# Seven block products for the down projections of a two-layer decoder trunk

## The chip, the cores and the metric

The kernel runs on one core of a Trainium2 chip. The metric is the device time of one execution in microseconds (us). TensorE (PE) multiplies; VectorE (DVE), ScalarE (ACT) and GpSimd (POOL) work on SBUF and PSUM; SyncE (SP) issues most DMAs.

## What is computed

1088 tokens (a prompt of 1024 and 8 samples of 8) go through two layers, each a token mixer and a ConvFFN, and a final norm. Everything is float32. Three of the products go from a wide row back to the 1024 features, and are added to x through a gate that depends on the sequence:

```python
def conv_ffn(h, past, w_up, conv_w, conv_b, w_down):
    a = h @ w_up                                   # 1024 -> 2 x 2816
    conv = sum(conv_w[j] * ap[:, j:j + T] for j in range(CONV_W)) + conv_b
    g, u = jnp.split(conv, 2, axis=-1)
    y = (jax.nn.silu(g) * u) @ w_down              # 2816 -> 1024
...
    out = (u * mixed.reshape(B, T, D_SGU)) @ w_out # 2048 -> 1024 (sgu_mix, layer 1)
...
    x = x + g1 * mix
    x = x + g2 * f                                 # after each mixer, each ConvFFN
```

Layer 0 has attention and a ConvFFN, layer 1 the spatial gating mixer (SGU) and a ConvFFN. So there are three down products: `w_down` of layer 0 (22 row tiles of 128), `w_sgu_out` (16), `w_down` of layer 1 (22).

## The kernel before

Activations lie feature-major: a row tile is 128 features by 1088 tokens. For float32 accuracy each operand is split in two float32r parts, high and low, and a product is three passes: high by high, high by low, low by high (`mm`, L370, issues each matmul; every matmul of the kernel has that line, and the name of its PSUM tile tells the stage: `m` the up product, `acc` the down product, `misc` a last block, `adaps` conditioning).

The up product of an FFN is already done in the seven-product (Winograd) form for all but its first column tiles: two blocks of columns, two of rows and two halves of the tokens make seven products in place of eight, in two parts z of 272 tokens a half. ACT and DVE add them from PSUM (`ev`, `ext`: L1544 to L1567), POOL makes the weights' sums and low parts (L1485 to L1502). Behind each pair of column tiles come the convolution (L1678, L1680, DVE), the gate (L1693) and the store of the row tile in a scratch tensor in DRAM (`pscr`; `sscr` for the SGU).

`Down.run` (L1625) does a down product in blocks of row tiles, `FF_BLOCKS = [4, 4, 4, 4, 2, 4]` and `SG_BLOCKS = [4, 4, 4, 4]`. For each block but the last, `proj_block` (L1196) goes over eight column tiles m of 128 features. A weight unit holds two of them (a *unit* below); it comes by DMA (`raw`), ACT casts it to `whi` (L305), and DVE (POOL for `w_sgu_out`) makes `wlo` (L312). For each m there are three chunks of tokens (384, 384, 320 columns), one PSUM bank each, and 3 passes for each row tile. Then `add_gated_` (L524 to L535) adds the banks to x with the gate, on DVE: one operation per bank and two small ones for the samples (`gs`, `xs`).

The rows of the next block are brought by `load` (L1587): a DMA of the row tile (`p`, L1594), the cast `gh` on ACT (L1596), the rest `gl` on DVE (L1597). The first four are loaded within the last up pair, as `free` gives back the tiles of the norm's rows, after its products 1, 2, 4 and 7; x comes back from `xscr` after the last (L1599). In layer 0 the 48 conditioning units of layer 1 are spread over the units of the first five blocks. The last block is done by `last_block7` (L1411; then another seven-product stage follows) or `last_block` (L1441), chunk by chunk, with the norm of the next stage behind it.

The order of work on each engine follows from the program text and from a priority (`tc.high_priority`) that puts the adds from PSUM ahead; each engine then runs its own queue in order. SBUF tiles of one row tile come from a ring of 37 slots (`slot`), weights from pools `raw` and `w`, PSUM tiles from 8 banks.

## Time and profile before

| | |
|---|---|
| time of three runs | 2646.1, 2651.22, 2651.64 us (median 2651.22) |
| profiled execution: its own time and its span | 2651.8 us, from its first to its last instruction |
| mean granted TensorE clock | 0.982 |
| busy: PE, DVE, ACT, POOL | 97%, 64%, 37%, 51% of the span |
| first down product up to its last block | 961.9 to 1205 us |
| SGU down product up to its last block | 1661.9 to 1810.9 us |
| last down product up to its last block | 2371.3 to 2589.7 us |

A row of a group gives line, engine, operation, `out<-in` by tile names, the shapes and the count, then after the bar the busy time in us and the mean of one in ns, and after the next bar the idle time ahead of it with what ended it. A row of the chain or the timeline gives start, duration, engine and what. A row of the windows gives, for a stretch, the busy time of PE, PE's weight loads, DVE, ACT and POOL with the count of instructions, then the granted clock, the DMA share and GB/s. PE's ends are modelled, so a busy PE is not PE at its peak.

### The profile page before, as it was taken

To read this page: it belongs to the slowest core of one execution; us is meant where nothing else is said; L and a number is where in the kernel's file an instruction comes from. 1 tells how busy PE (TensorE), PEld (TensorE's weight loads), DVE (VectorE), ACT (ScalarE), POOL (GpSimd) and SP (SyncE) were. 2 spreads that over 40 slices of the span, in tenths; PEclk is the share of its full clock that TensorE was granted. 3 is DMA by queue.
4 is the path that set the end of the run, shared out by engine and by line. 5 is a ranking of instruction groups with operands and counts; after the bars stand their busy time and mean duration, and the time that the engine had idled before them with its cause. 6 is when DMAs were issued, how large, how long until landed. Compare 5 with 4: busy or idle time off the path is not lost.

```text
span 2651.8 us, 45949 instructions
## 1 busy us (share of the span) xinstructions
PE 2559.8 (97%) x17916; PEld 2393.3 (90%) x17916; DVE 1687.4 (64%) x3336; ACT 976.8 (37%) x1971; POOL 1358.2 (51%) x1456
## 2 busy tenths in 40 slices
PE   7999999979999999999999999999979999999998
PEld 5676788979999999999788999999879999999998
DVE  5415867877767774446744555655886777766545
ACT  3216853433343331113325655212533343332203
POOL 2315634589999920002543766223489999950002
PEclk9999999989999999999999999999889999999999
DMA  8242213012222265443322434521212222244211
GB/s 295 92 157 97 69 58 120 25 52 80 88 76 74 82 258 189 179 175 130 105 82 78 158 131 160 204 80 64 72 38 78 90 74 74 74 166 176 96 44 68
DMA packets 113945, 292.21 MB, mean 110 GB/s; under 512 B 15329, under 2 KB 47137, under 8 KB 113697
## 3 DMA queue, kind: packets, MB, share of 16 engines
q1 hardware_dynamic: 82016, 232.49, 26.5%
q10 hardware_dynamic: 31712, 56.79, 5.6%
q8 instruction: 142, 2.33, 0.4%
q14 instruction: 75, 0.61, 0.1%
HBM read 228.06 MB, written 63.07 MB: 110 GB/s over the span
## 4 chain that ended last, share of the span: by engine, by line
PE 80%; DVE 11%; POOL 4%; ACT 2%; issue 2%; DMA 1%; SPq 0%; DVEq 0%; ACTq 0%; POOLq 0%
PE m L370 31%; PE acc L370 23%; PE misc L370 8%; PE v L370 7%; PE y L370 5%; POOL w L1485 2%; PE u L370 2%; PE adaps L370 2%; DVE cv L1678 1%; DMA raw<-wts 1%; DVE cv L1680 1%; DVE ha L1348 1%; PE pv L370 1%; ACT P L836 1%; DVE T L1364 1%
## 5 line engine op out<-in xcount | busy, mean ns | idle before, releaser
L370 PE MATMUL m<-th,w 128*128 128x272 f32 x2944 | 568.2, 290 | 25.5 <-ACT ext L1702 18.7
L370 PEld LDWEIGHTS m<-th,w 128*128 128x128 f32 x2944 | 469.8, 190 | 26.3 <-ACT ext L1702 19.1
L370 PE MATMUL m<-tl,w 128*128 128x272 f32 x1472 | 426.9, 290 | 0.0
L531 DVE SCALAR_TENSOR_TENSOR x<-acc,mod,x 128x384 f32<-128x384 f32 (+1 forms) x312 | 159.6, 568 | 239.9 <-PE acc L370 233.8
L370 PE MATMUL m<-hb,w 128*128 128x272 f32 x2208 | 293.2, 289 | 0.0
L370 PEld LDWEIGHTS m<-hb,w 128*128 128x128 f32 x2208 | 284.5, 189 | 0.0
L370 PEld LDWEIGHTS m<-tl,w 128*128 128x128 f32 x1472 | 280.1, 190 | 0.0
L370 PE MATMUL acc<-gh,whi 128*128 128x384 f32 (+1 forms) x1152 | 256.2, 330 | 1.1 <-DVE mixed L1934 0.8
L305 ACT CAST whi<-raw 128x1024 fp32r<-128x1024 f32 (+1 forms) x112 | 113.9, 1018 | 386.8 <-PE acc L370 221.5
L370 PE MATMUL acc<-gl,whi 128*128 128x384 f32 (+1 forms) x1152 | 253.8, 328 | 0.6 <-DVE gl L1597 0.6
L370 PE MATMUL acc<-gh,wlo 128*128 128x384 f32 (+1 forms) x1152 | 253.6, 328 | 0.0
L1295 POOL TENSOR_TENSOR nsq<-nsq 128x544 f32<-128x544 f32 x36 | 55.7, 1547 | 308.2 <-ACT nsq L1288 271.5
L370 PEld LDWEIGHTS acc<-gh,whi 128*128 128x128 f32 x1152 | 195.0, 188 | 10.0 <-issue 5.8
L1485 POOL TENSOR_TENSOR w<-raw,w 128x512 fp32r<-128x512 f32 x138 | 189.1, 1382 | 28.5 <-ACT w L1484 27.2
L370 PEld LDWEIGHTS acc<-gl,whi 128*128 128x128 f32 x1152 | 195.9, 188 | 0.9 <-DVE gl L1597 0.9
L370 PEld LDWEIGHTS acc<-gh,wlo 128*128 128x128 f32 x1152 | 195.8, 188 | 0.0
L1678 DVE SCALAR_TENSOR_TENSOR cv<-ext,cst,cv 128x1104 f32<-128x1104 f32 x88 | 129.0, 1501 | 86.9 <-ACT cv L1677 40.4
L1484 ACT CAST w<-Sa 128x512 fp32r<-128x512 f32 x92 | 56.9, 623 | 309.4 <-POOL Sa L1495 163.1
L1544 DVE TENSOR_TENSOR ext<-ev,m 128x272 f32<-128x272 f32 (+1 forms) x456 | 137.7, 338 | 48.5 <-PE m L370 39.4
L312 POOL TENSOR_TENSOR wlo<-raw,whi 128x1024 fp32r<-128x1024 f32 x28 | 69.7, 2490 | 186.4 <-ACT whi L305 169.3
L1680 DVE SCALAR_TENSOR_TENSOR cv<-ext,cst,cv 128x1104 f32<-128x1104 f32 x88 | 160.9, 1862 | 0.1
L370 PE MATMUL m<-ha,w 128*128 128x272 f32 x1104 | 151.5, 294 | 9.4 <-ACT ext L1702 9.4
(279 smaller groups left out, 5775.3 us busy)
## 6 DMA issues: line engine op xcount, KB each, us to landing
raw<-wts SPq DMA_DIRECT2D x244, 512.0 KB, 3.8
wada<-wts SPq DMA_DIRECT2D x48, 512.0 KB, 4.2
pscr<-cv ACTq DMA_DIRECT2D x44, 544.0 KB, 5.5
p<-pscr SPq DMA_DIRECT2D x40, 544.0 KB, 6.0
xscr<-x ACTq DMA_DIRECT2D x24, 512.0 KB, 2.6
x<-xscr SPq DMA_DIRECT2D x24, 512.0 KB, 8.3
sscr<-mixed ACTq DMA_DIRECT2D x16, 544.0 KB, 3.6
vscr<-v ACTq DMA_DIRECT2D x32, 256.0 KB, 2.6
```

The lines of the kernel that those rows point to most:

```text
L305: nc.scalar.copy(hi[:, :c], r[:, :c])
L312: eng.tensor_sub(lo[:, :c], r[:, :c], hi[:, :c].bitcast(F32))
L370: PE.matmul(out, lhsT=l, rhs=r, start=start, stop=stop)
L531: V.scalar_tensor_tensor(xv, p[:, 0:w], gp, xv, op0=ALU.mult, op1=ALU.add)
L836: A.activation(p, p, AF.Exp, bias=nm[:, h:h + 1], scale=0.125, accum_out=su[:, h:h + 1])
L1295: (V if m == 7 else G).tensor_add(s.ss[z], s.ss[z], q)
L1348: V.scalar_tensor_tensor(lo, t[:, h, 0:w], sh, hi.bitcast(F32), op0=ALU.add, op1=ALU.subtract)
L1484: A.copy(t[:, 0:512], src)
L1485: eng.tensor_sub(t[:, 512:1024], src, t[:, 0:512].bitcast(F32))
L1544: V.tensor_add(o, f(p), f(q))
L1678: V.scalar_tensor_tensor(t[:, 0:1104], e[:, 1:1105], cw(jj * 3 + 1), t[:, 0:1104], op0=ALU.mult, op1=ALU.add)
L1680: V.scalar_tensor_tensor(t[:, 0:1104], e[:, 0:1104], cw(jj * 3), t[:, 0:1104], op0=ALU.mult, op1=ALU.add)
```

## The change

All blocks of the three down products but the last are done as seven block products too. The blocks of one product are two row tiles (A, B), two halves of the tokens, and the two column tiles of a weight unit.

- `Rows` loads a pair of row tiles as `pr`, makes four sums (`tr`, 544 columns each: on DVE for the first pairs, on POOL for the others) and splits seven sides into high and low parts: seven casts on ACT, seven subtractions on DVE (L1590, L1596).
- `weights` makes the seven weights of a unit (a new layout, key `o7`): four sums of 256 columns on POOL (L1659 to L1668), four casts on ACT, four subtractions on DVE of 512, 256, 512 and 512 columns (L1656); half of that for a block of two row tiles. It is a generator, one step of it after each product of the unit before. These units are no longer fetched by `prefetch` or `ahead`.
- `run` does the products of a unit in the order 1, 5, 4, 6, 2, 3, 7, with product 4 put off into the next unit. Each product is two parts z of 272 columns and sums over the block's pairs. Three pairs of PSUM banks are used: `acA` (1, then 6 and 7, and 4), `acC` (5, 3), `acB` (2); a later product goes on in the bank of an earlier one, and the bank is added again after each.
- The banks are added without the gate to `acc`, eight tiles in SBUF: twelve adds of 272 columns on DVE a unit (L1729), and product 1 by a copy on ACT and an add on POOL. In the first block ACT copies the banks of the products that come first.
- `merge` brings x back and adds `acc` with the gate (L1688, and `gs`, `xs`, L1691, L1693), two column tiles a unit in the last seven-product block and two behind it.
- `free` now starts the first pair after product 2 of the last up pair and the second after product 7. The scratch tensors are laid out by halves of the tokens, the SGU's gate writes that layout, and conditioning weights come from the ring of slots. The last blocks are as before.

```diff
-LA, LB = 3, 5
+LA, LB = 1, 2
...
+            if k == "o7":
+                a = a.reshape(nk // 2, 2, 128, 2, 128).transpose(2, 1, 3, 0, 4)
+                a = np.stack([a[:, 0, 0], a[:, 1, 0], a[:, 1, 1], a[:, 0, 1]], 1)
...
+        def make(r):
+            a, b = r.p
+            V_, e = V.tensor_sub, r.e.tensor_sub
+            t1 = slot([128, 2, 544], name="tr")
+            e(t1[:, 0], a[:, 1], a[:, 0])
+            e(t1[:, 1], b[:, 1], t1[:, 0])
+            h0 = slot([128, 2, 544], F32R, name="h0")
+            A.copy(h0[:, 0], a[:, 0])
+            V_(h0[:, 1], a[:, 0], h0[:, 0].bitcast(F32))
...
+            e(t2[:, 0], b[:, 1], a[:, 1])
+            e(t2[:, 1], b[:, 0], t1[:, 1])
...
+            G.tensor_add(S1, A21, A22)
+            parts(f[:, 0:2 * n], 1, 2)
+            yield
+            G.tensor_sub(S2, S1, A11)
+            parts(f[:, 2 * n:3 * n], 4)
+            yield
+            parts(sf[:, 0:2 * n], 5, 6)
+            G.tensor_sub(S4, A12, S2)
+            yield
+            G.tensor_sub(S3, A11, A21)
+            yield
+            parts(sf[:, 2 * n:4 * n], 3, 7)
...
                 elif i == 2:
                     for k in range(1, 8, 2):
                         norm.ab[k][0] = None
-                    s.load(1)
-                elif i == 4:
-                    s.load(2)
+                    s.pair(0, V)
                 elif i == 7:
                     norm.th = norm.tl = None
-                    s.load(3)
-                    s.load_x()
+                    if s.blocks[0] > 2:
+                        s.pair(1, V)
...
+            def add(m, h, b, first, z, e=None):
+                o = s.acc[m][:, h, z * 272:z * 272 + 272]
+                p = b[z][:, 0:272]
+                if first:
+                    A.copy(o, p)
+                elif e:
+                    t = sm.tile([128, 272], F32, name="ev", tag="ev", bufs=4)
+                    A.copy(t, p)
+                    e.tensor_add(o, o, t)
+                else:
+                    V.tensor_add(o, o, p)
...
+                        if i == 1:
+                            product(w, sd, bA, True, lambda z: add(m0, 0, bA, first, z, G))
+                        elif i == 5:
+                            product(w, sd, bC, True, lambda z: add(m1, 1, bC, first, z))
+                        elif i == 4:
+                            while late:
+                                late.pop(0)()
+                            late.append(lambda w=w, sd=sd, bA=bA, m1=m1, first=first:
+                                        product(w, sd, bA, False, lambda z: add(m1, 0, bA, first, z)))
+                        elif i == 6:
+                            product(w, sd, bA, False, lambda z: add(m0, 1, bA, first, z))
+                        elif i == 2:
+                            product(w, sd, bB, True, lambda z: add(m0, 0, bB, False, z))
+                        elif i == 3:
+                            product(w, sd, bC, False, lambda z: add(m0, 1, bC, False, z))
+                        elif i == 7:
+                            product(w, sd, bA, False, lambda z: add(m1, 1, bA, False, z))
...
+                        if i == 4 and b == nb - 2 and u > 0:
+                            s.merge(2 * u - 2)
+                            s.merge(2 * u - 1)
```

How the queues change shows on DVE. First the transition to the third down product: before, the convolution and the gate of the last pair with the loads' subtractions (`gl`) between them, ahead of the last up products' adds (`ev`).

```order
L1678 SCALAR_TENSOR_TENSOR cv<-ext,cst,cv 128x1104 x2
L1680 SCALAR_TENSOR_TENSOR cv<-ext,cst,cv 128x1104 x2
L1597 TENSOR_TENSOR gl<-p,gh 128x1088
L1693 TENSOR_TENSOR cv<-cv 128x1024
L312 TENSOR_TENSOR wlo<-raw,whi 128x1024
L1694 TENSOR_TENSOR cv<-cv 128x64
L1544 TENSOR_TENSOR ext<-ev,m 128x272
L1544 TENSOR_TENSOR ext<-ev,m 128x240
L1544 TENSOR_TENSOR ext<-ev,m 128x4x8
L1597 TENSOR_TENSOR gl<-p,gh 128x1088
L1561 TENSOR_TENSOR ev<-ev,m 128x272 x2
L1565 TENSOR_TENSOR ev<-ev,m 128x272
```

Now, DVE's queue from the first pair's sums (`tr`) on, again up to the adds of the last up products; the convolution's operations come 20 rows further on.

```order
L1586 TENSOR_TENSOR tr<-pr 128x544
L1656 TENSOR_TENSOR w_26887<-raw,w_26887 128x512
L1587 TENSOR_TENSOR tr<-pr,tr 128x544
L1656 TENSOR_TENSOR w_26917<-raw,w_26917 128x256
L1590 TENSOR_TENSOR h_26861<-pr,h_26861 128x544
L1596 TENSOR_TENSOR h_26865<-tr,h_26864 128x544 x2
L1600 TENSOR_TENSOR tr<-pr 128x544
L1602 TENSOR_TENSOR tr<-pr,tr 128x544
L1596 TENSOR_TENSOR h_26874<-pr,h_26873 128x544 x2
L1596 TENSOR_TENSOR h_26880<-tr,h_26879 128x544 x2
L1554 TENSOR_TENSOR ev<-ev,m 128x272 x2
L1656 TENSOR_TENSOR w_26948<-s_26885,w_26948 128x512
```

The first pair's eleven operations and three weight subtractions stand ahead of the last up pair's `ev` adds. The queue goes on with the second pair and the convolution, up to the first unit's adds from `acB`:

```order
L1596 TENSOR_TENSOR h_27043<-tr,h_27042 128x544 x2
L1537 TENSOR_TENSOR ext<-ev,m 128x272
L1537 TENSOR_TENSOR ext<-ev,m 128x240
L1537 TENSOR_TENSOR ext<-ev,m 128x4x8
L1656 TENSOR_TENSOR w_27137<-raw,w_27137 128x512
L1656 TENSOR_TENSOR w_27172<-raw,w_27172 128x256
L1656 TENSOR_TENSOR w_27189<-s_27135,w_27189 128x512
L1656 TENSOR_TENSOR w_27222<-s_27135,w_27222 128x512
L1843 SCALAR_TENSOR_TENSOR cv<-ext,cst,cv 128x1104 x2
L1845 SCALAR_TENSOR_TENSOR cv<-ext,cst,cv 128x1104 x2
L1729 TENSOR_TENSOR acc_27097<-acc_27097,acB 128x272
```

The second pair's last subtractions, four of a weight unit and the four of the convolution stand ahead of the first `acc` add. In the middle of the third product, a unit before (two column tiles, one subtraction of the weights, one of a row tile per column tile):

```order
L535 TENSOR_TENSOR xs<-xs,gs 128x64
L1597 TENSOR_TENSOR gl<-p,gh 128x1088
L531 SCALAR_TENSOR_TENSOR x_25739<-acc,mod,x_25739 128x384 x2
L531 SCALAR_TENSOR_TENSOR x_25739<-acc,mod,x_25739 128x256
L534 TENSOR_TENSOR gs<-acc,mod 128x64
L535 TENSOR_TENSOR xs<-xs,gs 128x64
L1597 TENSOR_TENSOR gl<-p,gh 128x1088
L531 SCALAR_TENSOR_TENSOR x_25741<-acc,mod,x_25741 128x384 x2
L531 SCALAR_TENSOR_TENSOR x_25741<-acc,mod,x_25741 128x256
L534 TENSOR_TENSOR gs<-acc,mod 128x64
L312 TENSOR_TENSOR wlo<-raw,whi 128x1024
```

And a stretch of the second block now, where `w_...` are weights' low parts, `h_...` rows' low parts (their sums are on POOL), and the `acc` adds read a bank:

```order
L1590 TENSOR_TENSOR h_27855<-pr,h_27855 128x544
L1729 TENSOR_TENSOR acc_27097<-acc_27097,acC 128x272 x2
L1656 TENSOR_TENSOR w_27845<-raw,w_27845 128x512
L1729 TENSOR_TENSOR acc_27098<-acc_27098,acA 128x272 x2
L1596 TENSOR_TENSOR h_27859<-tr,h_27858 128x544 x2
L1596 TENSOR_TENSOR h_27868<-pr,h_27867 128x544
L1729 TENSOR_TENSOR acc_27240<-acc_27240,acC 128x272
L1596 TENSOR_TENSOR h_27868<-pr,h_27867 128x544
L1729 TENSOR_TENSOR acc_27240<-acc_27240,acC 128x272
L1596 TENSOR_TENSOR h_27874<-tr,h_27873 128x544 x2
L1729 TENSOR_TENSOR acc_27098<-acc_27098,acA 128x272 x2
L1656 TENSOR_TENSOR w_27894<-raw,w_27894 128x256
```

The three wide operations of x for each column tile are now narrow adds to `acc`, twelve a unit, with subtractions of weights and rows between them. Last, the block of two row tiles in the third product, where the merges (L1688) stand between the adds; before, this place looked like the unit shown above.

```order
L1729 TENSOR_TENSOR acc_27240<-acc_27240,acA 128x272 x2
L1729 TENSOR_TENSOR acc_27396<-acc_27396,acC 128x272 x2
L1656 TENSOR_TENSOR w_29562<-raw,w_29562 128x256
L1729 TENSOR_TENSOR acc_27240<-acc_27240,acA 128x272 x2
L1656 TENSOR_TENSOR w_29581<-raw,w_29581 128x128
L1688 SCALAR_TENSOR_TENSOR x_29584<-acc_27239,mod,x_29584 128x1024
L1691 TENSOR_TENSOR gs<-acc_27239,mod 128x32 x2
L1688 SCALAR_TENSOR_TENSOR x_29591<-acc_27240,mod,x_29591 128x1024
L1693 TENSOR_TENSOR xs<-xs,gs 128x64
L1691 TENSOR_TENSOR gs<-acc_27240,mod 128x32 x2
L1729 TENSOR_TENSOR acc_27395<-acc_27395,acA 128x272
L1693 TENSOR_TENSOR xs<-xs,gs 128x64
```

A merge and its small operations stand between the adds of one unit and those of the next.

More of the change, by code (lines that the diff above doesn't have):

```diff
@@ L282, in dma @@
         elif key[0] == "ada" and key[1] == 1:
-            t = s.wp.tile([128, 1024], F32, name="wada", tag="w")
+            t = s.first()
         else:
@@ L367, in build, with mm @@
     ws.first = lambda: slot([128, 1024], name="raw0")
-    def mm(out, l, r, start, stop):
-        PE.matmul(out, lhsT=l, rhs=r, start=start, stop=stop)
+    def mm(out, l, r, start, stop, more=False):
+        PE.matmul(out, lhsT=l, rhs=r, start=start, stop=stop, skip_group_check=more)
     cT = cp.tile([128, 8, 9], F32, name="cT")
@@ L1609, in f @@
                         norm.ab[k] = None
-                    s.load(0)
                 elif i == 2:
@@ L1626, in run @@
             nb = len(s.blocks)
[L1627 to L1643 removed]
+            bk = {}
@@ new lines, in run, with product @@
+            late = []
+            def add(m, h, b, first, z, e=None):
[7 more added lines that the diff above has]
+                    e.tensor_add(o, o, t)
+                else:
+                    V.tensor_add(o, o, p)
+            def product(w, sides, b, start, post):
+                for z in range(2):
+                    o = b[z][:, 0:272]
+                    n, tot = 0, 3 * len(sides)
+                    for q, sd in enumerate(sides):
+                        for wl, xl in ((0, 0), (0, 1), (1, 0)):
+                            mm(o, w[wl][:, q * 128:q * 128 + 128], sd[xl][:, z * 272:z * 272 + 272],
+                               start and n == 0, n == tot - 1, not start)
+                            n += 1
+                    post(z)
@@ L1646, in extra @@
                         stage(2)
-                        for _ in ada_fill(4 * b + m // 2):
+                        for _ in ada_fill(4 * b + u):
                             ada_unit()
                             ws.ahead(2)
-                proj_block(h_, l_, s.g, extra)
+                del rows
+            late.pop(0)()
+            s.merge(6)
+            s.merge(7)
+            del W
+            ks = range(s.starts[nb - 1], s.starts[nb])
+            h_, l_ = [s.h.pop(k) for k in ks], [s.l.pop(k) for k in ks]
+            flush()
+            if s.ada:
+                norm.g, norm.s = mods[1, SC1], mods[1, SH1]
+            (last_block7 if s.seven else last_block)(h_, l_, s.g, norm)
     def ffn(l, norm, nxt):
@@ L1656, in ffn @@
         cw, cb = cv("conv_w", l, 132), cv("conv_b", l, 44)
-        ps_scr = dp.tile([NJ, 128, T], F32, name=f"pscr{l}")
+        ps_scr = dp.tile([NJ, 128, 2, 544], F32, name=f"pscr{l}")
         def ext(jj):
@@ L1768, in ffn @@
                 W1 = gen = None
-                pair(norm, W, place, lambda: ws.ahead(1), down.free(norm))
+                pair(norm, W, place, down.prep, down.free(norm))
             tg = conv(e[0], j)
@@ L1960, in build @@
             W1 = gen = None
-            pair(norm, W, place, lambda: ws.ahead(1), down.free(norm))
+            pair(norm, W, place, down.prep, down.free(norm))
         W = W1
```

201 lines of the change are left out of this document (133 added, 68 removed).

## The prediction

> **What bounds the kernel now.** I read the page first, then the chain of waits, then the busy times by stage.
>
> ```profile
> PE 2559.8 (97%) x17916; PEld 2393.3 (90%) x17916; DVE 1687.4 (64%) x3336; ACT 976.8 (37%) x1971; POOL 1358.2 (51%) x1456
> ...
> core 0: 2651.8 us, clock 0.982
> ```
>
> TensorE is busy for 97% of the span, and DVE for only 64%. A share over the whole span says little about three stages, so the next view is the chain through the first and the third down product.
>
> ```profile
> 949.89 12.04 PE m L370 x96
> ...
> 973.87 1.00 PE adaps L370 x16
> 974.87 12.13 PE acc L370 x72
> ...
> 2379.26 210.45 PE acc L370 x1266
> 2589.72 22.80 PE misc L370 x120
> ```
>
> Nothing but TensorE stands on it from the first matmul of the product to its last block: 72 matmuls of a weight unit of four row tiles (12.13 us), then conditioning matmuls in layer 0. The busy times over the three products (first, spatial gating, third) say how much room the others have:
>
> ```profile
> core 0: us, PE busy (x) PEld busy (x) DVE busy (x) ACT busy (x) POOL busy (x), PEclk, DMA share, GB/s
> 961.90:1205.00 243.10, 243.10 (x1692) 225.82 (x1690) 127.95 (x263) 45.61 (x48) 1.84 (x5) 1.00 0.56 201
> 1661.90:1810.90 149.00, 148.17 (x903) 147.29 (x902) 84.75 (x149) 28.08 (x27) 28.84 (x12) 1.00 0.36 128
> 2371.30:2589.70 218.40, 217.53 (x1311) 216.78 (x1310) 126.57 (x252) 43.23 (x43) 2.80 (x5) 1.00 0.32 116
> ```
>
> TensorE is full at granted clock 1.00, DVE is at 53 to 58%, POOL nearly empty. The change spends that room; the question is whether it is enough.
>
> **TensorE: what goes.** The up stage already runs 272-column matmuls: 96 in 12.04 us, 0.1254 us each. A seven-product unit of four row tiles has 7 products x 2 token parts x 2 row pairs x 3 passes = 84 of them: 10.54 us in place of 12.13, 1.59 saved. The first and the third product have 18 such units each (16, and four half-size ones that count as two), the gating product 12. The gain is 28.6 + 19.1 + 28.6 = 76.3 us, if TensorE stays the limit.
>
> **DVE in a steady unit.** Durations by form, and one pair of adds back to back from the timeline:
>
> ```profile
> L1567 DVE TENSOR_TENSOR ev<-ev,m 128x272 f32<-128x272 f32 x92 | 40.2, 437 | 50.1 <-PE m L370 50.1
> L312 DVE TENSOR_TENSOR wlo<-raw,whi 128x512 fp32r<-128x512 f32 x8 | 5.5, 684 | 0.0
> L312 DVE TENSOR_TENSOR wlo<-raw,whi 128x1024 fp32r<-128x1024 f32 x76 | 94.0, 1241 | 47.9 <-ACT whi L305 46.6 <-PE acc L370 0.9
> L1597 DVE TENSOR_TENSOR gl<-p,gh 128x1088 fp32r<-128x1088 f32 x60 | 80.6, 1344 | 35.9 <-ACT gh L1596 35.8
> ...
> 2347.97 0.79 DVE L1544 TENSOR_TENSOR ext<-ev,m 128x272 f32<-128x272 f32 x2
> ```
>
> Twelve adds of a 272-column PSUM bank: 12 x 0.437 = 5.2 us alone, 4.3 back to back (0.79 for two, so 0.36 for each that follows). Four weight subtractions, three of 512 columns and one of 256: 512 to 1024 columns cost 1.09 ns a column, so 256 is about 0.41, and the four are 2.46. Row splits, seven of 544 columns (0.72 by the same slope) to a pair of row tiles and two pairs to a block of four units: 3.5 x 0.72 = 2.5. Together 9.3 to 10.2 us against 10.54: DVE fits, with almost nothing over.
>
> **POOL, and what it shares.** POOL gets four weight sums of 256, half of four row sums of 544, and two adds of 272 for product 1.
>
> ```profile
> L857 POOL TENSOR_TENSOR q<-qT,q 128x256 fp32r<-128x256 f32 x32 | 23.4, 735 | 6.1 <-ACT q L856 6.1
> ...
> 2339.34 1.96 DVE L1693 TENSOR_TENSOR cv<-cv 128x1024 f32<-128x1024 f32 x1
> ...
> 2340.18 2.28 POOL L1495 TENSOR_TENSOR Sa<-Sa,raw 128x512 f32<-128x512 f32 x1
> 2342.54 1.30 POOL L1502 TENSOR_TENSOR Sb<-raw,Sa 128x512 f32<-128x512 f32 x1
> ...
> 2360.62 1.22 DVE L1693 TENSOR_TENSOR cv<-cv 128x1024 f32<-128x1024 f32 x1
> ```
>
> 4 x 0.735 = 2.9; 2 x 1.38 (1.30 at 512 columns, 2.2 ns a column) = 2.8; 2 x 0.77 = 1.5: 7.2 us, well under 10.54 by itself. But the rows show that it isn't by itself. DVE's product of two SBUF tiles takes 1.96 us while POOL sums, and 1.22 when POOL is idle; POOL's sum of 512 takes 2.28 beside it and 1.30 when DVE is reading PSUM. The two-input operations on SBUF run one after the other. The Trainium skill, "SBUF — State Buffer", section "Who interferes with whom", has this as a rule: DVE's second input and GpSimd go through one shared port pair, held for a whole instruction, and a DVE operation with one SBUF input stays clear of it. The trace agrees (1.96 against 1.22). So the sum that counts is DVE's two-SBUF operations, 2.46 + 2.5 = 5.0, and POOL's 7.2: 12.2 us a unit at most against TensorE's 10.54. At the low end none of it matters, since buffers let the engines run apart. I take the middle, 0.83 us a unit, in the units that make rows for later blocks: about ten in an FFN product, six in the gating product. That is +8 in the third, +5 in the gating product, and +3 in the first, where conditioning matmuls stand between the units:
>
> ```profile
> L370 PE MATMUL adaps<-wada,cp 128*32 128x256 f32 x384 | 24.9, 384 | 0.0
> ```
>
> 24.9 us over 20 units are 1.2 a unit, in which DVE and POOL catch up. Ends of this term over all three: 0 and 1.66 x 26 = 43.
>
> **The start of each product.** Before, the first rows need one cast and one subtraction each. Now the first unit needs both pairs of the block: the second pair is asked for when the seventh up product has given its tiles back. Rows of the transition to the third product, and of the gap inside the gating stage where TensorE stops today:
>
> ```profile
> 2354.30 2.65 DVE L1678 SCALAR_TENSOR_TENSOR cv<-ext,cst,cv 128x1104 f32<-128x1104 f32 x2 [1.85 <-issue]
> 2356.86 2.64 DVE L1680 SCALAR_TENSOR_TENSOR cv<-ext,cst,cv 128x1104 f32<-128x1104 f32 x2
> ...
> 2363.47 6.58 DMA p<-pscr
> ...
> 1689.94 10.07 PE acc L370 x60
> ...
> 1701.57 0.13 DVE gs L534
> 1701.70 2.83 DVE gl L1597
> 1704.53 0.14 DVE xs L535
> ...
> 1705.25 105.68 PE acc L370 x638
> ```
>
> A pair made on DVE is 4 sums and 7 subtractions, 11 x 0.64 to 0.72 = 7.0 to 7.9 us, after a landing of 6.58. The seven sides come out one by one, so TensorE can follow after the first; against that four convolution operations (5.3 us) and a unit's weight subtractions stand in DVE's queue ahead of the first unit's adds from PSUM, and the second unit's product 5 waits for a bank of those. Least: the landing alone, 7. Most: 6.6 + 7 + 5.3 + 2.5 = 21. I take 15 for the third product, 11 for the first, where the first conditioning matmuls follow the unit. The gating product has no convolution behind it: 11, less the 5 us for which TensorE waits there now (from 1700.0, the end of the 60 matmuls, to 1705.25): 6.
>
> **The end.** In the two FFN products the last seven-product block has two row tiles: 5.27 us of TensorE a unit, but DVE still has 12 adds (4.3 to 5.2), four subtractions of half size (1.5), a row load (1.34) and two merges. A merge is a 1024-column operation on two SBUF tiles (nearest row 1.22) and three small ones (0.13 to 0.14 in the rows above), 1.6 each. That is 10.4 to 11.3 us a unit, 20 to 24 us over in four units. The last block's first chunk (96 matmuls of 416 columns, 18.5 us at the same rate per column) needs no merged x itself, but its adds into x stand in the same DVE queue; I let it hide 13 of the 22: +9 in the third product, +4.5 in the first, whose conditioning covers 1.2 a unit. In the gating product this block has four row tiles (10.54): DVE has 4.3 + 2.5 + 1.34 + 3.2 = 11.3, up to 12.2: +4. Ends over all three: 0 and 45.
>
> **The queues that the moved steps pass.** SP issues the new weight units and the rows in order, and a row load that waits for a tile holds the weight load behind it; the loads of x wait for tiles too.
>
> ```profile
> p<-pscr SPq DMA_DIRECT2D x40, 544.0 KB, 6.0
> raw<-wts SPq DMA_DIRECT2D x244, 512.0 KB, 3.8
> x<-xscr SPq DMA_DIRECT2D x24, 512.0 KB, 8.3
> ...
> L1484 ACT CAST w<-raw 128x512 fp32r<-128x512 f32 x138 | 84.6, 618 | 77.4 <-PE m L370 69.3 <-DMA raw<-wts 6.6 <-PE v L370 1.5
> L1555 ACT COPY ev<-m 128x272 f32<-128x272 f32 x92 | 29.7, 372 | 0.0
> ```
>
> A weight unit lands in 3.8 us and needs 2.9 of POOL and 2.46 of DVE before its last product: 9.2 in a row, hidden by the 10.5 of the unit before; without that cover each unit would lose up to 9. A load of x (8.3) is hidden by a block's products; where one lands late, a merge waits at the head of DVE's queue with PSUM adds behind it, which the upper end holds. ACT gets the casts of the same tiles (0.618 per 512, about 2.2 for weights and 2.3 for rows a unit) and two copies of 0.372: 5.2 of 10.54, so nothing.
>
> **The sum.** Third: -28.6 + 15 + 8 + 9 = +3.4. First: -28.6 + 11 + 3 + 4.5 = -10.1. Gating: -19.1 + 6 + 5 + 4 = -4.1. All: -10.8. The profiled span, 2651.8 us, lies 0.6 above the median, 2651.2, so the forecast is 2640 us.
>
> **The rivals.**
>
> *TensorE stays the limit.* For it: in the up stage POOL is nearly full and DVE at 75%, and TensorE doesn't stop.
>
> ```profile
> 600.00:700.00 100.00, 100.00 (x795) 100.00 (x794) 75.11 (x115) 40.41 (x60) 97.40 (x97) 0.99 0.24 76
> ```
>
> Against it: there DVE's operations mostly read PSUM or have only the up stage's slack to meet, and the start and end don't have that cover at all. Port terms 0, starts and ends halved (25 us): 76 - 25 = 51, some 2600.
>
> *The start costs more than it gives (slower).* The first pair's sums stand in DVE's queue ahead of the last up products' adds from PSUM. If its rows land after the up banks have filled (four products of 24 matmuls, 3.0 us each), TensorE stops within the up stage too: about 7 us, and then the full chain of 21 in both FFN products and 16 in the gating product. 28 + 28 + 16 = 72 in place of 32: +40, about 2680.
>
> *The shared port sets every unit (slower).* DVE's queue is in order: a subtraction that waits for POOL's sum holds the PSUM adds behind it. With DVE at 10.2 and half of POOL's 7.2 added as waits, a unit takes about 13.8, 1.7 over the old 12.13, in the 26 units that make rows: the gain there, 41 us, becomes a loss of 44, and the rest of the sum stays, with the port terms of 16 taken out: -10.8 - 16 + 85 = +58 at worst, 2709. It brings the whole to zero at an excess of 1.0 a unit; two thirds of it, 57, give +30, 2681.
>
> *The clock drops after the gaps at the starts.* After a gap at the end of the gating product TensorE is granted half speed for a while, and after one as long at another place it is not:
>
> ```profile
> 1860.00:1870.00 10.00, 6.46 (x45) 5.79 (x44) 9.93 (x20) 4.42 (x10) 4.29 (x3) 0.87 0.42 158
> 1870.00:1880.00 10.00, 7.72 (x34) 6.74 (x34) 8.48 (x21) 3.67 (x9) 3.18 (x1) 0.50 0.40 159
> ...
> 1290.00:1300.00 10.00, 6.54 (x26) 4.36 (x25) 10.00 (x17) 3.11 (x7) 8.27 (x8) 1.00 0.01 2
> ```
>
> A spell costs some 0.5 x 7.7 + 0.13 x 6.5 = 5 us. Three of them put the forecast at 2655. The Trainium skill, "TensorE: Matmul & The Clock Gate", section "What's actually happening", has such a drop come after an idle window of about 3.4 us that runs free of the program, which fits one gap of two.
>
> **How the numbers follow.** A measurement of this kernel tells about 0.2%, 5.3 us, from no change: same is 2645.9 to 2656.5. The forecast (0.45, own range 2622 to 2660) splits into 0.29 faster, 0.10 same, 0.06 slower. TensorE the limit: 0.17, faster. Start: 0.15, slower. Port: 0.14, slower. Clock: 0.09, of it 0.05 same, 0.03 slower, 0.01 faster. Faster 0.47, same 0.15, slower 0.38. The range leaves out the best of the second case and the worst of the port's: 2603 to 2690.
>
> **What would show it.** Right: units of 10.5 to 11.4 us in the middle of the products, gaps of TensorE of 10 to 15 us at the starts with releaser DVE, stops in the block of two row tiles released by DVE's merges. Wrong: units of 10.54 without a gap (first rival), TensorE idle inside the last up pair (second), units over 12 with DVE's subtractions lengthened to twice 0.68 (third), a granted clock of 0.5 after a start (fourth).

## The result and the profile after

The changed kernel takes 2716.7 us (median of four runs, 2711.3 to 2722.0) against 2648.7 for the kernel before beside it: 1.0249 times, 95% interval 1.0225 to 1.0273. The forecast was 2640, the range ended at 2690. The profiled executions have spans of 2709.5 and 2651.8 us. The page of the changed kernel, its first line of busy times and its spans:

```profile
PE 2540.4 (94%) x18492; PEld 2357.2 (87%) x18492; DVE 1975.1 (73%) x3744; ACT 1136.7 (42%) x2423; POOL 1724.4 (64%) x1760
...
core 0: 2709.5 us, clock 0.968
```

TensorE is busy for 19 us less, in a span that is 58 us longer, at a lower granted clock. Where this happens is seen by stage. The busy times from the end of the up products to the start of the next stage, for the first, the gating and the third down product with their last blocks: first the kernel before, then the changed one.

```profile
961.90:1256.50 294.60, 294.60 (x2102) 277.12 (x2101) 161.00 (x345) 65.75 (x86) 19.27 (x16) 1.00 0.52 186
1662.10:1861.70 199.60, 198.77 (x1310) 197.70 (x1309) 117.18 (x214) 45.58 (x59) 52.93 (x26) 1.00 0.32 115
2373.00:2641.90 268.90, 268.01 (x1616) 266.02 (x1615) 152.95 (x317) 60.91 (x91) 21.66 (x24) 1.00 0.28 101
```

```profile
956.70:1274.70 318.00, 288.48 (x2317) 262.17 (x2316) 253.21 (x495) 124.16 (x248) 160.04 (x147) 0.95 0.51 178
1681.30:1892.70 211.40, 189.66 (x1453) 185.84 (x1454) 182.44 (x322) 86.84 (x169) 112.88 (x89) 0.97 0.32 112
2399.10:2698.70 299.60, 265.28 (x1832) 258.38 (x1831) 255.20 (x468) 120.71 (x254) 169.89 (x155) 0.93 0.29 93
sum 829.00, PE 743.42 PEld 706.40 DVE 690.85 ACT 331.72 POOL 442.81; mean PE 247.81 PEld 235.47 DVE 230.28 ACT 110.57 POOL 147.60
```

The three stages take 829.0 us in place of 763.1, 66 more. TensorE is idle in them for 829.0 - 743.4 = 85.6 us, against 1.7 before. And the granted clock, 1.00 in all three before, is 0.95, 0.97 and 0.93. By the trace's record it is either full or half, and some 85 us of the stages passed at half (the rows give 2 x (0.05 x 318 + 0.03 x 211 + 0.07 x 300) = 86). TensorE was busy in 67 of these, so the clock costs about half of that, 33 us. DVE is busy for 80 to 86% of a stage, so nothing is full by its mean.

Outside the three stages the changed kernel is 8 us shorter (1880.5 against 1888.7); e8 below shows where that comes from. The idle time lies in the middle of the products more than at their starts. The same view of the changed kernel, the first 45 us of each stage, then what lies between those and the last 90 us (sums alone):

```profile
sum 135.00, PE 105.76 PEld 99.32 DVE 119.48 ACT 78.13 POOL 81.36; mean PE 35.25 PEld 33.11 DVE 39.83 ACT 26.04 POOL 27.12
```

```profile
sum 424.00, PE 378.18 PEld 360.07 DVE 348.52 ACT 161.84 POOL 254.80; mean PE 126.06 PEld 120.02 DVE 116.17 ACT 53.95 POOL 84.93
```

29 us at the starts, 46 in the middle, and 10.5 in the last 90 us (270.0 less 259.5 by the same view). In the middle of the third product, TensorE's waits are nearly all for one thing, the adds of the banks on DVE (the view of waits, who for whom: us in total, times, the longest):

```profile
PE acA L378 <- DVE acc L1729: 13.7, 7, 3.4
PE acA L378 <- ACT ev L1726: 1.6, 1, 1.6
PE acC L378 <- DVE acc L1729: 1.0, 2, 0.8
```

What DVE does in such a wait is shown by the timeline of the first product around 1138 us, DVE first, then POOL, then the matmul that waited:

```profile
1134.96 2.89 DVE L1596 TENSOR_TENSOR h<-tr,h 128x544 fp32r<-128x544 f32 x2
1137.78 0.42 DVE L1729 TENSOR_TENSOR acc<-acc,acC 128x272 f32<-128x272 f32 x1
1138.12 1.53 DVE L1596 TENSOR_TENSOR h<-pr,h 128x544 fp32r<-128x544 f32 x1
1139.57 0.42 DVE L1729 TENSOR_TENSOR acc<-acc,acC 128x272 f32<-128x272 f32 x1
1139.92 1.50 DVE L1596 TENSOR_TENSOR h<-pr,h 128x544 fp32r<-128x544 f32 x1
1141.35 1.91 DVE L1596 TENSOR_TENSOR h<-tr,h 128x544 fp32r<-128x544 f32 x2
1143.18 1.47 DVE L1729 TENSOR_TENSOR acc<-acc,acA 128x272 f32<-128x272 f32 x4
```

```profile
1136.01 1.26 POOL L1727 TENSOR_TENSOR acc<-acc,ev 128x272 f32<-128x272 f32 x1
1137.23 1.83 POOL L1600 TENSOR_TENSOR tr<-pr 128x544 f32<-128x544 f32 x1
1139.03 1.81 POOL L1602 TENSOR_TENSOR tr<-pr,tr 128x544 f32<-128x544 f32 x1
1140.80 1.24 POOL L1727 TENSOR_TENSOR acc<-acc,ev 128x272 f32<-128x272 f32 x1
```

```profile
1143.66 1.73 PE L378 MATMUL acB<-h,w 128*128 128x272 f32 x6 [4.83 <-DVE acc L1729]
```

The subtractions of a pair (`h`) and POOL's sums for the same pair take turns: a subtraction takes 1.5 us beside a sum, and each ends about 0.6 us after the sum that ran beside it. Of the last two, one has POOL's add of product 1 beside it (1.28) and one has POOL idle:

```profile
1142.55 0.71 DVE L1596 TENSOR_TENSOR h<-tr,h 128x544 fp32r<-128x544 f32 x1
```

The adds that read PSUM take 0.42 either way. The adds of `acA` stand at the end of this queue. The second part of product 2 (`acB`) needs a bank that the first of them gives back, and TensorE waits 4.83 us for it. (Product 1 reaches POOL through a copy on ACT, `ev`: no POOL operation of the three stages reads a bank.) The groups by form show the same in the mean:

```profile
L1596 DVE TENSOR_TENSOR h<-tr,h 128x544 fp32r<-128x544 f32 x96 | 98.3, 1051 | 8.6 <-ACT h L1595 7.7
L1729 DVE TENSOR_TENSOR acc<-acc,acC 128x272 f32<-128x272 f32 x184 | 74.8, 429 | 31.8 <-PE acC L378 31.3
L1602 POOL TENSOR_TENSOR tr<-pr,tr 128x544 f32<-128x544 f32 x18 | 33.4, 1855 | 0.0
L1727 POOL TENSOR_TENSOR acc<-acc,ev 128x272 f32<-128x272 f32 x80 | 77.4, 980 | 77.3 <-ACT ev L1726 77.2
```

A subtraction takes 1.05 us in the mean where the prediction reckoned 0.72. A row sum takes 1.86 in the dearest of its four lines (shown) and 1.66 in the mean of all 72, where it reckoned 1.38. The adds are at 0.43 as reckoned.

### The profile page after: what moved, and what is told of

It is laid out like the page before. It is cut to its first block, busy times and chain, and to the rows that moved or that the text cites. A ratio compares the mean times of both kernels' runs of the same rounds, so it can differ in the third digit from the quotient of the medians.

```text
span 2709.5 us, 48657 instructions
## 1 busy us (share of the span) xinstructions
PE 2540.4 (94%) x18492; PEld 2357.2 (87%) x18492; DVE 1975.1 (73%) x3744; ACT 1136.7 (42%) x2423; POOL 1724.4 (64%) x1760
## 4 chain that ended last, share of the span: by engine, by line
PE 70%; DVE 19%; issue 4%; ACT 3%; POOL 2%; DMA 2%; SPq 0%; DVEq 0%; ACTq 0%; POOLq 0%
PE m L378 33%; PE misc L378 7%; PE acA L378 7%; PE v L378 6%; PE y L378 5%; DVE h L1596 3%; PE acC L378 3%; DVE acc L1729 2%; PE u L378 2%; PE acB L378 2%; DVE w L1656 1%; PE adaps L378 1%; PE acc L378 1%; DMA raw<-wts 1%; DVE ha L1341 1%
## 5 line engine op out<-in xcount | busy, mean ns | idle before, releaser
L378 PE MATMUL acA<-h,w 128*128 128x272 f32 x2304 | 343.2, 303 | 62.4 <-DVE acc L1729 41.8
L378 PEld LDWEIGHTS acA<-h,w 128*128 128x128 f32 x2304 | 317.3, 199 | 82.1 <-DVE acc L1729 47.0
L378 PE MATMUL acC<-h,w 128*128 128x272 f32 x1152 | 172.3, 298 | 7.1 <-DVE acc L1729 7.0
L378 PEld LDWEIGHTS acC<-h,w 128*128 128x128 f32 x1152 | 159.2, 198 | 10.9 <-DVE acc L1729 10.2
L378 PEld LDWEIGHTS m<-ha,w 128*128 128x128 f32 x1104 | 144.9, 193 | 16.0 <-ACT ext L1867 15.5
L1659 POOL TENSOR_TENSOR s<-raw 128x256 f32<-128x256 f32 (+1 forms) x52 | 47.4, 911 | 173.7 <-PE acB L378 69.7
L1478 POOL TENSOR_TENSOR w<-Sb,w 128x512 fp32r<-128x512 f32 x92 | 136.6, 1503 | 17.6 <-ACT w L1477 17.5
L1727 POOL TENSOR_TENSOR acc<-acc,ev 128x272 f32<-128x272 f32 x80 | 77.4, 980 | 77.3 <-ACT ev L1726 77.2
L1842 ACT ACTIVATE cv<-ext,cst 128x1104 f32<-128x1104 f32 x88 | 111.3, 1306 | 28.6 <-POOL ext L1828 15.3
L1478 POOL TENSOR_TENSOR w<-Sa,w 128x512 fp32r<-128x512 f32 x92 | 119.8, 1319 | 5.2 <-ACT w L1477 5.2
```

What stands on the lines that cost most here:

```text
L378: PE.matmul(out, lhsT=l, rhs=r, start=start, stop=stop, skip_group_check=more)
L1478: eng.tensor_sub(t[:, 512:1024], src, t[:, 0:512].bitcast(F32))
L1659: G.tensor_add(S1, A21, A22)
L1727: e.tensor_add(o, o, t)
L1842: A.activation(t[:, 0:1104], e[:, 2:1106], AF.Identity, scale=cw(jj * 3 + 2), bias=cb(jj))
```

## The experiments

The theory (A): DVE's and POOL's operations on two SBUF tiles exclude each other, and their sum is too long in the units that make a pair of rows. Rivals: (B) DVE's queue alone, with a pair's subtractions ahead of the adds; (C) the starts; (D) POOL's results come late. The table has the medians, the ratio to the kernel before on the same chip, and the three stages' sum from the windows of each run's profile. The kernel before took 2648.7 to 2655.4 us on the chips of these runs, so differences of medians under some 6 us say little; there the ratios decide.

| run | us | ratio to before (95%) | three stages |
|---|---|---|---|
| changed kernel | 2716.7 | 1.0249 (1.0225 to 1.0273) | 829.0 |
| e1 no row sums on POOL | 2639.4 | 0.9947 (0.9928 to 0.9966) | 765.5 |
| e2 no row subtractions on DVE | 2666.9 | 1.0047 (1.0032 to 1.0062) | 787.5 |
| e3 product 1 on DVE | 2703.8 | 1.0194 (1.0161 to 1.0227) | 822.6 |
| e4 no weight sums on POOL | 2670.8 | 1.0064 (1.0041 to 1.0086) | 788.4 |
| e5 pairs spread over a block | 2672.3 | 1.0067 (1.0042 to 1.0092) | 793.4 |
| e6 e5 and e3 | 2660.4 | 1.0023 (1.0008 to 1.0037) | 779.7 |
| e7 light first pairs | 2693.6 | 1.0149 (1.0122 to 1.0176) | 807.1 |
| e8 before, with the new store alone | 2637.9 | 0.9939 (0.9926 to 0.9951) | 761.3 |
| e9 e6, a plain block first | 2648.8 | 0.9982 (0.9968 to 0.9995) | 768.1 |
| e10 memsets for row sums | 2652.7 | 1.0006 (0.9996 to 1.0015) | 769.8 |
| e11 e9, copies on DVE too | 2651.1 | 1.0005 (0.9992 to 1.0019) | 769.2 |
| e12 no POOL work | 2626.9 | 0.9920 (0.9895 to 0.9946) | 744.8 |

**e1, row sums left out.**

```diff
-            e(t1[:, 0], a[:, 1], a[:, 0])
-            e(t1[:, 1], b[:, 1], t1[:, 0])
+            if r.e is V:
+                e(t1[:, 0], a[:, 1], a[:, 0])
+                e(t1[:, 1], b[:, 1], t1[:, 0])
+            else:
+                t1 = a
...
```

> The changed kernel takes 2716.7 us; TensorE's gaps in the middle of the three products are 51 us of it and half-clock spells 37. Left out: POOL's four sums for each pair of row tiles that is made for a later block (the row itself is split in place of the sum); the DVE subtractions of those pairs stay. Theory A (DVE's and POOL's operations on two SBUF tiles exclude each other, so it is their sum that is too long): 2.8 us of 12.2 a unit go, DVE's row subtractions fall from 1.05 to about 0.8 us in the mean, most gaps in the middle and two thirds of the half-clock spells go, 2640 to 2665 us. Theory B (DVE's queue is in order and the seven subtractions of a pair stand ahead of the adds from PSUM, whatever POOL does): the gaps stay, 2700 to 2717 us. Theory C (the starts of the products cost most): 2705 to 2717 us.

2639.4 us, 77 less and just past the good end of A's range. B and C, which gave 2700 or more, fall.

**e2, row subtractions left out.**

```diff
...
-                    V_(l[:, i], f[:, i], h[:, i].bitcast(F32))
+                    if r.e is V:
+                        V_(l[:, i], f[:, i], h[:, i].bitcast(F32))
+                    else:
+                        A.copy(l[:, i], f[:, i])
```

> Left out: DVE's seven subtractions for each pair of row tiles that is made for a later block (the low part is a copy on ACT instead); POOL's sums stay. Theory A (sum of DVE's and POOL's two-tile operations): 2.5 us of 12.2 a unit go, about as much as when POOL's sums go, 2640 to 2665 us. Theory B (the burst of subtractions in DVE's queue): all gaps in the middle and their half-clock spells go, 2635 to 2650 us, far more than without POOL's sums. Theory C (the starts): 2705 to 2717 us.

2666.9 us, 50 less, 2 above A's range. To take 2.5 us a unit off DVE gives less than 2.8 off POOL, where B had far more, so DVE's own queue isn't what decides. The comparison isn't quite clean: the copies that stand in for the subtractions keep ACT busy for 396 us of the stages in place of 332.

**e3, product 1 added by DVE.**

```diff
-                            product(w, sd, bA, True, lambda z: add(m0, 0, bA, first, z, G))
+                            product(w, sd, bA, True, lambda z: add(m0, 0, bA, first, z))
```

> Product 1 is added from PSUM by DVE (two adds more a unit, 0.36 to 0.43 us each) in place of a copy on ACT and an add on POOL. The computation is whole. Theory A: POOL's two adds of 0.98 us in the mean leave the shared time, the new adds read PSUM and don't share it, so a unit gets 1.2 to 2 us of room for 0.8 of DVE: 2690 to 2705 us. Theory B (DVE's queue is the limit): 0.8 us more on DVE in the units that are full, 2717 to 2740 us.

2703.8 us: 13 less with more work on DVE, the fuller of the two engines. B had it slower. The intervals of the two ratios just touch; e6 takes the same step from another kernel and gains the same.

**e4, weight sums left out.**

```diff
-            sf = wp.tile([128, 1024], F32, name="s7", tag="w")
+            sf = f
-            G.tensor_add(S1, A21, A22)
...
-            G.tensor_sub(S2, S1, A11)
...
```

> Left out: POOL's four sums of 256 columns for a unit's weights (the blocks themselves are split in place of the sums). Theory A: 2.9 us of 12.2 a unit go, also in the units that make no rows, 2635 to 2665 us. Theory B (burst of row subtractions on DVE): 2695 to 2717 us. A third way, D (POOL's chain of four row sums is late and the rows come late): POOL gets to the rows earlier, 2680 to 2700 us, with less from this run than from leaving out the row sums.

2670.8 us, 46 less: below D's range, 6 above A's. The stages say where: 27.5 us less in the third product (272.1 in place of 299.6), 9.6 in the gating product, and only 3.5 in the first. There the gap of 4.8 us around 1140 us stays, with no weight sum near it: a pair's sums and subtractions are enough by themselves once they come in one burst.

**e5, the pairs spread.** `make` becomes a generator that gives way after each sum and each split, and `run` takes a step of it after each product.

```diff
-                        if u0 <= u < u0 + len(nq):
-                            todo.append(lambda q=nq[u - u0]: s.pair(q, G))
...
+                        if nx is not None and u >= u0:
+                            want = tot * ((u - u0) * 7 + ORDER.index(i) + 1) // ((4 - u0) * 7 - LEAVE)
+                            while done < want:
+                                next(nx, None)
+                                done += 1
...
```

> The computation is whole and no work is left out: the row pairs for the next block are made step by step, one sum or split after each product over all four units of a block, in place of a whole pair within one unit. Theory A1 (the shared port, and the sum is too long in the two units of a block that each make a whole pair: 7 subtractions and 4 sums there, 17 us of two-tile work beside 10.5 of TensorE, against 12.2 in the mean of the block): gaps in the middle fall from 44 us to 10 to 20, half-clock spells by a third, 2655 to 2690 us. Theory A2 (the shared port over the whole block, 12.2 in each unit on average, is what counts): spreading moves the gaps and keeps them, 2705 to 2717 us.

2672.3 us, 44 less, with every operation still there: within A1's range, where A2 had no gain. The middle of the stages by the same view as above:

```profile
sum 388.40, PE 358.34 PEld 340.58 DVE 342.69 ACT 158.62 POOL 248.78; mean PE 119.45 PEld 113.53 DVE 114.23 ACT 52.87 POOL 82.93
```

TensorE is idle there for 30 us in place of 46, not the 10 to 20 that A1 gave, and the half-clock loss of the three stages falls from 33 us to about 20. So the sum within the unit that makes a pair counts, but it isn't all: the mean over the block, 12.2 us against 10.54, is too long as well (e6, where POOL's adds of product 1 go out of it, brings the 30 to 18). The step also asks for the rows earlier. Late rows don't look like the limit in the middle of the changed kernel, though: in TensorE's gaps of 0.9 us or more there, DVE is busy throughout (in one of them for 92%).

**e6, both e5 and e3.**

> As the run with the pairs spread over the block, and product 1 is added from PSUM by DVE in place of ACT and POOL. Whole computation. Theory A1: 10 to 13 us under the spread run, as the change of product 1 gave alone (13 us). Theory A2: DVE has 0.8 us a unit more in units that are already full everywhere, no gain over the spread run or a loss of up to 10 us.

2660.4 us, 12 less than e5, as A1 had it. The subtractions, by form, fall from 1.05 us to 0.94:

```profile
L1603 DVE TENSOR_TENSOR h<-tr,h 128x544 fp32r<-128x544 f32 x96 | 88.2, 935 | 2.4 <-ACT h L1602 2.4
```

**e7, light first pairs.** DVE's sums and subtractions for the pairs of the first block are left out.

```diff
-            e(t1[:, 0], a[:, 1], a[:, 0])
+            if r.e is G:
+                e(t1[:, 0], a[:, 1], a[:, 0])
...
+                    if r.e is G:
+                        V_(l[:, i], f[:, i], h[:, i].bitcast(F32))
...
```

> Left out: all of DVE's work for the pairs of the first block (four sums and seven subtractions each; the rows themselves and their high parts stand in); loads and ACT's casts stay. Theory S1 (at the starts DVE's work on the first pairs is what TensorE waits for): start gaps fall from 36 us to about 10 and some half-clock time with them, 2670 to 2690 us. Theory S2 (the landing of the rows after the last up products' tiles are given back is what TensorE waits for): 2705 to 2717 us.

2693.6 us: 23 less, between S1's 27 to 47 and S2's 0 to 12. In the first 45 us of the stages TensorE's idle time falls only from 29 to 21 us (S1 had about 10), and the half-clock loss there by 4 to 5; the rest of the gain lies further on. So DVE's work on the first pairs is a part of the starts, and not the larger one. The 21 us that stay are waits for ACT's copies of the first block's banks (11.0) and for DVE's adds (9.8). The landing of the rows was not tried by itself.

**e8, the kernel before with the change's store alone.** The page of before had a row that the prediction passed over:

```profile
L1695 POOL COPY cv<-cv 128x64 f32<-128x64 f32 x44 | 12.6, 285 | 64.4 <-DVE cv L1694 64.2
```

POOL waits 64 us over the run at the head of its queue for DVE's gate. The edit takes POOL's copy out and stores the row tile by two DMAs, in the layout of before.

```diff
-            G.tensor_copy(tg[:, SEQ:T], tu[:, 0:64])
-            A.dma_start(ps_scr[j], tg[:, 0:T])
+            A.dma_start(ps_scr[j][:, 0:SEQ], tg[:, 0:SEQ])
+            A.dma_start(ps_scr[j][:, SEQ:T], tu[:, 0:64])
```

> The kernel before with one edit that the change carries along: the FFN's gate no longer lets POOL copy the samples' 64 columns behind the prompt's before the store; the row tile is stored by two DMAs. Whole computation. Theory U (the 8 to 9 us by which each up stage is shorter in the changed kernel come from this: POOL's copy waits for DVE's gate, 64 us of idle time over the run, with the next weights' sums queued behind it): 2630 to 2642 us against 2649 to 2655 before. Theory V (they come from another part of the change, such as the order of the first steps or fewer weights in the pools): within 4 us of before.

2637.9 us, 15 less than before beside it, and the fastest kernel of the study that leaves nothing out. The two up stages with what stands ahead of them, before and in e8:

```profile
sum 849.40, PE 814.59 PEld 813.78 DVE 618.79 ACT 331.57 POOL 776.90; mean PE 407.30 PEld 406.89 DVE 309.39 ACT 165.79 POOL 388.45
```

```profile
sum 838.70, PE 811.72 PEld 811.24 DVE 622.17 ACT 331.14 POOL 769.04; mean PE 405.86 PEld 405.62 DVE 311.09 ACT 165.57 POOL 384.52
```

10.7 us less (the changed kernel has 838.1). The gain that U gave came; its mechanism is not shown. Of the 64 us, 58 lie in four waits where the up stages end, with no weight sums of the up product left to make, and 3.2 near the beginning of each. What is gone from the up stages is one wait of TensorE in each for DVE's add of `ext` (L1544; 4.3 and 2.5 us), with the half-clock spell of 3.4 us behind it, and 1 us of the gaps at the first one's start. How the store brings that about stays open. Since the up stages of the changed kernel are as short as e8's, the rest of the change costs about 2716.7 - 2637.9 = 79 us, and the store hides 15 of it.

**e9, a plain block first.** `FF_BLOCKS` has the block of two row tiles first; it is done with plain products in four chunks of 272 columns, its banks copied to `acc` by ACT, while the next block's pairs are made.

```diff
-FF_BLOCKS = [4, 4, 4, 4, 2, 4]
+FF_BLOCKS = [2, 4, 4, 4, 4, 4]
...
+                if b == 0 and s.plain:
...
+                            for c in range(4):
+                                A.copy(s.acc[m][:, c // 2, c % 2 * 272:c % 2 * 272 + 272], bp[c][:, 0:272])
...
```

> As the run with spread pairs and product 1 on DVE (2660 us), but in the two FFN products the block of two row tiles comes first and is done in the plain form, its banks copied to acc by ACT, while the pairs of the next block are made; the four other blocks have four row tiles. Whole computation. Theory S (the starts, 10 us of gaps and about 5 of half clock in each FFN product, come from making the first pairs with nothing to do for TensorE): 15 us less in each, 3.2 back for the plain form: 2630 to 2645 us. Theory P (the gaps move to the next block, since the sum of DVE's and POOL's work is what it was): 2655 to 2670 us.

2648.8 us, 12 less than e6, between S's range and P's. The third product gains 11 (268.6 in place of 279.8), the first nothing (297.0 and 297.1): there TensorE now waits 7.0 us for ACT's copies of the conditioning sums.

**e10, memsets in place of the row sums.**

```diff
+            if r.e is G:
+                def e(o, i, j):
+                    for v in range(NSET):
+                        G.memset(o, float(v))
...
```

> The changed kernel, with each of POOL's row sums (544 columns, 1.36 us alone) for later blocks replaced by three memsets of the same tile, which read nothing and take POOL about as long (0.53 us for 512 columns). Left out: the sums themselves. DVE's subtractions stay. Theory A (what costs is that POOL's sums read SBUF while DVE needs its second input): DVE's row subtractions fall to 0.75 us or less beside them, 2635 to 2660 us, as without the sums (2639). Theory D (what costs is that POOL is busy for so long and hands its results on late): 2690 to 2717 us, as with the sums.

2652.7 us, 64 less, though POOL is nearly as long in this work (109.7 us, where the 72 sums took 119.7). The groups by form:

```profile
L1588 POOL MEMSET tr<- 128x544 f32 x216 | 109.7, 555 | 1.4 <-PE acA L378 0.8
L1600 DVE TENSOR_TENSOR h<-tr,h 128x544 fp32r<-128x544 f32 x96 | 76.7, 829 | 11.0 <-ACT h L1599 10.7
```

DVE's subtractions fall from 1.05 to 0.83 us. That is somewhat above the 0.75 that A gave, but it is what they take in e1, where POOL has nothing in place of the sums (0.84). D falls: a busy POOL that reads nothing from SBUF leaves DVE alone. The 13 us to e1 may be POOL's occupation, later weight sums for one; that was not taken apart. The memsets also don't wait for a row's landing as the sums do, so a part of the gain could be theirs.

**e11, half of the plain block's copies on DVE.**

```diff
-                                A.copy(s.acc[m][:, c // 2, c % 2 * 272:c % 2 * 272 + 272], bp[c][:, 0:272])
+                                (V.tensor_copy if c % 2 else A.copy)(s.acc[m][:, c // 2, c % 2 * 272:c % 2 * 272 + 272], bp[c][:, 0:272])
```

> As the run with the plain block of two row tiles first (2649 us), with half of that block's banks copied to acc by DVE in place of ACT. Whole computation. Theory Q (in that block TensorE waits 3.4 us a product for ACT's copies, which stand behind casts and behind a store's issue that waits for the gate): 2638 to 2645 us. Theory P (the wait moves to DVE, which stands behind the convolution): 2645 to 2655 us.

2651.1 us: P holds, nothing gained. TensorE's waits in the plain blocks are 8.2 us for DVE's copies and none for ACT's, where e9 had 6.9 for ACT's.

**e12, no POOL work in the blocks.** The edits of e1, e3 and e4 together.

> All of POOL's work in the seven-product blocks is gone: left out are the row sums for later blocks and the weights' sums (the blocks and rows themselves are split in their place); product 1 is added from PSUM by DVE. DVE keeps every subtraction and has 14 adds a unit. Theory A (the shared time is what bounds the middle; DVE alone, 5 us of adds and 5 of subtractions a unit against 10.54, is not): gaps in the middle fall to 5 us or less, what is left are the starts, the ends and their half-clock time, 2605 to 2630 us. Theory F (DVE alone is full, so it is the limit as soon as POOL isn't): 2635 to 2650 us, no better than leaving out the row sums alone (2639).

2626.9 us; F falls. With POOL idle a subtraction takes what the prediction reckoned:

```profile
L1600 DVE TENSOR_TENSOR h<-pr,h 128x544 fp32r<-128x544 f32 x120 | 80.8, 719 | 0.4 <-ACT h L1599 0.2
```

Even so the three stages take 744.8 us against 761.3 in e8: 16 less, where the matmuls alone would give 69. TensorE is idle for 3 us in the middle, as A had it, but for 17 at the starts and 12 in the last 90 us.

## Why the prediction was wrong

**The gain** was mis-sized first, if by little. The prediction took 12.13 us for a plain unit, a row of the first product. Its own row of the third, 210.45 us for 1266 matmuls, gives 0.1662 each and 11.97 for 72, so the gain is 1.43 a unit, and 69 us over 48 units in place of 76. The new matmuls are what the prediction took them for: at full clock 3561 of 3715 steps from one of the blocks' matmuls to the next are 0.12 or 0.13 us. The other 154 are about twice as long and hold 19 us; they look like waits too short for the profile to show as idle time.

**The shared port** is the step that failed. The prediction saw the exclusion, had its rows, and then took "the middle, 0.83 us a unit, in the units that make rows for later blocks", from a sum of 12.2 us that spreads two pairs over four units. The change makes a whole pair in one unit: there DVE has 7 subtractions x 0.72 + 2.46 = 7.5 us of two-tile work and POOL 2.9 + 4 x 1.38 + 1.5 = 9.9, together 17.4 against TensorE's 10.54. The other units of the block don't give it back. That TensorE can't run ahead of the adds, since a unit takes six of the eight banks, is argued from the program and was not tried. Measured idle in the middle: 46 us for a term of 16. e5, which moves the same work apart, brings it to 30 and takes 44 us off the whole; so to halve the excess of 1.66 us a unit (43 us in all) was too kind as well. Without the row sums (e1) 9 are left, without any POOL work (e12) 3.

**The clock** was a rival of 5 us a spell at three starts, outside the sum. It fell after many gaps in the middle as well, and costs some 33 us, two fifths of the idle time. The record of the clock changes on a grid of 3.41 us alone. A stretch of the third product, window by window of that grid, with gaps of 3.0 and 3.4 us at 2525.6 and 2541.5 us:

```profile
2523.30:2526.70 3.40, 2.33 (x19) 2.11 (x17) 3.40 (x4) 1.99 (x4) 3.31 (x4) 1.00 0.62 187
2526.70:2530.10 3.40, 1.46 (x11) 1.46 (x12) 3.40 (x8) 0.09 (x1) 3.32 (x4) 1.00 0.16 34
2530.10:2533.50 3.40, 3.40 (x17) 3.40 (x16) 3.40 (x6) 1.47 (x4) 1.34 (x2) 0.50 0.32 128
2533.50:2537.00 3.50, 3.50 (x30) 3.50 (x29) 3.50 (x5) 1.66 (x4) 3.14 (x3) 1.00 0.00 0
2537.00:2540.40 3.40, 3.25 (x26) 3.03 (x24) 3.40 (x6) 1.48 (x3) 3.32 (x3) 1.00 0.00 0
2540.40:2543.80 3.40, 1.01 (x6) 0.80 (x6) 3.40 (x5) 0.76 (x2) 3.32 (x4) 0.99 0.00 0
2543.80:2547.20 3.40, 2.36 (x10) 2.37 (x11) 3.40 (x10) 0.00 (x0) 0.35 (x1) 0.50 0.71 230
2547.20:2550.60 3.40, 3.40 (x17) 3.40 (x16) 2.25 (x5) 1.31 (x3) 0.77 (x1) 0.50 0.23 93
2550.60:2554.00 3.40, 3.40 (x29) 3.40 (x28) 1.59 (x4) 0.61 (x2) 0.77 (x1) 1.00 0.52 154
```

A window in which TensorE is busy for 2.33 us (69%) leaves the clock full, one of 1.46 (43%) is followed by half, and half lasts until a window is busy throughout. It is so in all three stages of the changed kernel. Of 218 windows at full clock, all 14 that were busy for 43% or less were followed by half clock, and of the 201 that were busy for 51% or more one was; between lie three (47 to 49%), of which one was. Half clock ended behind each window of 88% or more and behind none of 73% or less. This tells the prediction's two places apart as well: the window ahead of the drop at 1867 us was busy for 48%, those around 1287 to 1297 us for 54% or more; neither place has a gap over 1.8 us. The clock was not tried by itself; in all runs it fell with the gaps (0.98 to 0.99 in e12's stages). The Trainium skill, "TensorE: Matmul & The Clock Gate", section "What's actually happening", has the clock fall after an idle window of about 3.4 us; the trace agrees on the window, but a window that is half busy is idle enough here, and so a gap of 2.1 us was enough at 1110 us.

**The starts** were forecast at 32 us net, with 5 us credited for a stop of TensorE in the gating stage; idle at the starts is 29 (11.4, 4.4 and 13.4 by stage, against 11, 6 and 15). That is near, and in part by luck. The credit was a misreading: the chain had DVE from 1700.0 to 1705.25, but a chain shows what released what, not that TensorE stood still, and the windows row of the same stage had TensorE busy for 148.17 of 149.00 us. And the prediction put ACT at nothing, but 12.6 of the 29 us are waits for ACT's copies of the first block's banks (L1723), most of them in one gap of the first product. The view of waits there, 956 to 1002 us, and what the copies stood behind on ACT:

```profile
PE acA L378 <- ACT acc L1723: 9.6, 2, 7.3
```

```profile
968.29 1.31 ACT L1842 ACTIVATE cv<-ext,cst 128x1104 f32<-128x1104 f32 x1 [3.78 <-POOL past L1851]
```

Two operations of the convolution are ahead of the copies in ACT's queue, and ACT waits 3.78 us for a small copy on POOL ahead of these. e7 shows DVE's part. (Of the three weight subtractions that the section on the change puts ahead of the last up products' adds, its list shows two; the third stands behind two of the adds.) **The ends** were forecast at 17.5; the last 90 us of the three stages hold 10.5 of idle time.

**The store** was not costed at all. It gave 11 us in the up stages and 15 in the whole (e8), by a way that stays open.

Put together by what was measured in the profile: -69 of matmuls, +84 of idle time, +33 of clock, +19 of long steps between matmuls, -8 outside the stages make +59, and the spans differ by 58. The clock and the steps are estimates from the trace, good to a few us.

Of the rivals, the shared port (2681, at worst 2709) and the clock both came, and the range took them one at a time. That TensorE stays the limit fell. The second rival, TensorE stopped within the last up pair, did not come: the up stages are no longer than in e8, 838.1 against 838.7.

## What to carry to other kernels

Fewer matmuls help only as far as the other engines' work for a unit fits in the shorter unit, and that sum is to be made for the fullest unit in the order as written, with DVE's and POOL's operations on two SBUF tiles added together. Spread the work before giving up the form (44 us here), but have the mean fit as well. Count the clock too: here each window of 3.41 us in which TensorE was busy for 43% or less was followed by 3.4 us or more at half speed. A change that carries a small edit along (here a store without POOL's copy) should be timed without the rest: that edit alone made the fastest kernel that leaves nothing out, 2637.9 us.

## What was not expected of the hardware

Three memsets on POOL beside DVE cost it nothing that can be seen (subtractions of 0.83 us, against 0.84 with nothing in their place), where one sum of about the same length cost it much (1.05 us in the mean, 1.5 in a burst): it is the reading of SBUF by POOL, not its being busy. The Trainium skill, "SBUF — State Buffer", section "Who interferes with whom", says that a DVE instruction with two SBUF inputs contends with a GpSimd instruction that reads SBUF and not with one that only writes it; e10 agrees.
